# Quarters of the first modulation vectors: x loaded ahead of the weights, three blocks interleaved, and a 0/1 matrix in place of two transposes

## The chip, the cores and the metric

The kernel runs on one core of a Trainium2 chip. The metric is the device time of one execution in microseconds (us), as the median of several runs. All profile rows below come from one profiled execution, recorded by the hardware profiler.

## What is computed

One inference step through two layers of a diffusion backbone on 640 tokens of 1024 features (512 latent tokens and 128 context tokens, each group with its own conditioning vector). Per layer:

```
m = silu(cond) @ w_ada + b_ada
sh1, sc1, g1, sh2, sc2, g2 = split(m, 6)
h = rmsnorm(x) * (1 + sc1) + sh1
z = h @ w_in
branches: gated linear attention (4 heads), gated convolution, Fourier mixing
x += g1 * W_o(sum_b sigmoid(G_b) * W_b_out(branch_b))
h = rmsnorm(x) * (1 + sc2) + sh2
x += g2 * (silu(h @ w_gate) * (h @ w_up2)) @ w_down
```

and a last norm. All weights are float32, and nearly all of the time goes into streaming them and multiplying by them.

## The kernel before, in words

Everything is feature-major: a tile has 128 features on its partitions and all T = 640 tokens along its rows, so x is eight tiles of 128x640. The tokens go in two halves of 320 (TH).

**The weight stream.** `make_plan` (L816) lists every weight in the order of its use; `_load` (L127 to L136) issues the loads of 512 KB on the queue of SyncE (SP) into six buffers called raw; a buffer is free again when `take` (L175) has handed its weight out or its split is done. `prefetch` (L186) splits the weights that come next, up to two ahead: `_split` makes a rounded high part on ScalarE (`whi`, ACT L140) and the rest on VectorE (`wlo`, DVE L141), three buffers each. A dense product is done in three matmuls, high by high, low by high and high by low, each with a 128x128 block as the loaded operand and 320 tokens moving. A block of 128 outputs over eight feature blocks and both halves is so 8 x 3 x 2 = 48 matmuls (`dense` L242, or `mm3h` L224 to L226 by halves). Two blocks that are neighbours in the plan go as a `pair` (L244) in 84 matmuls by the scheme of Strassen and Winograd. It needs sums of the two halves of the tokens, which `token_sums` makes once per h: L290 to L293 on DVE, a high part `thi` on ACT (L301) and a low part `tlo` on DVE (L302).

**Modulation vectors.** They are made by pieces, a quarter of one vector at a time: 256 features for both conditioning vectors. `ada_mm` (L342) does 8 float32 matmuls with 32 columns loaded and 256 moving; their parts come out on four groups of 32 partitions, of which two rows each count. `ada_end` copies the 128x256 result to SBUF (ACT L348), transposes it in two blocks of 128x128 on TensorE (L351, `ident` is the identity), adds the four parts up with a reduction (DVE L354), adds b_ada (L355), and for the two scales makes A = (1 + sc) * norm (L358). It is called one piece late: `ada` does the products of a piece, then ends the piece before. There are 48 pieces: 8 in the start (sc1 and sh1 of layer 0, four quarters each), and 40 that the plan spreads among the pairs of the mixers and the FFN.

**The start** (`start`, L546). The stream's first six loads are issued, then x's eight. The first pieces are made while the norm is computed (squares on ACT and DVE, sum over features on PE at L409, 1/rms on ACT at L381), x is multiplied by it in eight DVE instructions (L565), and then, quarter by quarter, h is made by two activations per feature block (ACT L577), split in high and low (`hhl`, ACT L457 and DVE L455, L458), and fed to one block of the input projection, Q0. With it go the products `gk` (L541) of the low-rank gates. Q1, K0 and K1 (two blocks of 128 columns each make up Q and K) follow as dense blocks in `mixer` (L894); the token sums stand behind the call for K0. The first pair, `w1p_4`, is V's first two blocks; `w1p_6` is the next pair.

Which instruction of the program stands where on each engine is decided by a scheduler from priorities in program order; tiles come from pools (47 units of SBUF, four PSUM tiles of two banks), and an engine runs its own instructions strictly in the order given.

## Time and profile before

| what | number |
|---|---|
| runs (us) | 2076.96, 2074.67, 2073.61; median 2074.67 |
| span of the profiled execution (us) | 2075.0 |
| time of the profiled execution beside its span | none is given; the span stands 0.3 above the median |
| TensorE matmul (PE) busy | 2012.5 us, 97% |
| weight load (PEld) busy | 1936.3 us, 93% |
| VectorE (DVE) busy | 1570.5 us, 76% |
| ScalarE (ACT) busy | 919.4 us, 44% |
| read and written in HBM | 227.69 MB and 26.74 MB |

Busy time of PE is from the start of a matmul to its modelled end, so neighbours overlap; how fast it runs is read from the starts of neighbours. A row of the timeline has its start in us from the start of the span, the busy time, the engine, the line, the operation, the tiles out<-in with their shapes, how many instructions are put together (x2), and, in brackets, how long the engine was idle before it and what ended that.

### The profile page before, as it was taken

To read this page: it belongs to the slowest core of one execution; us is meant where nothing else is said; L and a number is where in the kernel's file an instruction comes from. 1 tells how busy PE (TensorE), PEld (TensorE's weight loads), DVE (VectorE), ACT (ScalarE), POOL (GpSimd) and SP (SyncE) were. 2 spreads that over 40 slices of the span, in tenths; PEclk is the share of its full clock that TensorE was granted. 3 is DMA by queue.
4 is the path that set the end of the run, shared out by engine and by line. 5 is a ranking of instruction groups with operands and counts; after the bars stand their busy time and mean duration, and the time that the engine had idled before them with its cause. 6 is when DMAs were issued, how large, how long until landed. Compare 5 with 4: busy or idle time off the path is not lost. (4 is left out here: it accounts for less than half of the span.)

```text
span 2075.0 us, 35216 instructions
## 1 busy us (share of the span) xinstructions
PE 2012.5 (97%) x14100; PEld 1936.3 (93%) x14100; DVE 1570.5 (76%) x2508; ACT 919.4 (44%) x1445; POOL 18.2 (1%) x52
## 2 busy tenths in 40 slices
PE   5999999999999999999999999999999999999997
PEld 2999998999999999999979999899999999999997
DVE  5778798877667777777677878898765787877876
ACT  5554435445445333333365454544543643333333
POOL 2000000000000000000000000000000000000000
PEclk9999999999999999999999999999999999999999
DMA  8254442554612333333232453335545222222222
GB/s 320 69 171 136 148 140 95 186 197 141 210 55 62 103 118 98 105 114 103 83 126 84 165 171 132 118 129 173 192 153 173 62 64 78 78 92 71 88 72 71
DMA packets 107139, 256.72 MB, mean 124 GB/s; under 512 B 13344, under 2 KB 46304, under 8 KB 106976
## 3 DMA queue, kind: packets, MB, share of 16 engines
q1 hardware_dynamic: 102528, 250.91, 36.8%
q8 instruction: 111, 1.82, 0.4%
q10 hardware_dynamic: 3728, 2.49, 0.4%
q0 software_dynamic: 720, 1.07, 0.1%
q14 instruction: 52, 0.43, 0.1%
HBM read 227.69 MB, written 26.74 MB: 123 GB/s over the span
## 5 line engine op out<-in xcount | busy, mean ns | idle before, releaser
L140 ACT CAST whi<-raw 128x1024 fp32r<-128x1024 f32 (+2 forms) x368 | 270.1, 734 | 529.5 <-PE wo L242 37.3
L141 DVE TENSOR_TENSOR wlo<-raw,whi 128x1024 fp32r<-128x1024 f32 (+2 forms) x368 | 304.4, 828 | 112.2 <-ACT whi L140 111.8
L242 PE MATMUL wd<-ffhi,whi 128*128 128x320 f32 x656 | 150.2, 310 | 0.0
L242 PE MATMUL wd<-fflo,whi 128*128 128x320 f32 x656 | 149.5, 309 | 0.0
L242 PE MATMUL wd<-ffhi,wlo 128*128 128x320 f32 x656 | 149.4, 309 | 0.0
L140 ACT CAST whi<-sb 128x1024 fp32r<-128x1024 f32 x86 | 90.3, 1050 | 125.7 <-PE wd L242 31.5
L140 ACT CAST whi<-sc 128x1024 fp32r<-128x1024 f32 x86 | 90.3, 1050 | 107.8 <-PE wd L242 48.0
L141 DVE TENSOR_TENSOR wlo<-sc,whi 128x1024 fp32r<-128x1024 f32 x86 | 104.9, 1220 | 30.2 <-ACT whi L140 29.6
L473 DVE SCALAR_TENSOR_TENSOR x<-wd,mod,x 128x512 f32<-128x512 f32 x212 | 106.7, 545 | 23.0 <-PE wd L242 23.0
L242 PEld LDWEIGHTS wd<-ffhi,whi 128*128 128x128 f32 x656 | 109.4, 188 | 3.3 <-ACT whi L140 3.3
L141 DVE TENSOR_TENSOR wlo<-sb,whi 128x1024 fp32r<-128x1024 f32 x86 | 104.8, 1219 | 6.8 <-ACT whi L140 6.7
L242 PEld LDWEIGHTS wd<-ffhi,wlo 128*128 128x128 f32 x656 | 109.7, 188 | 0.0
L242 PEld LDWEIGHTS wd<-fflo,whi 128*128 128x128 f32 x656 | 109.6, 188 | 0.0
L162 DVE TENSOR_TENSOR sc<-raw 128x512 f32<-128x512 f32 x86 | 59.3, 689 | 27.3 <-DMA raw<-in_w 26.0
L342 PE MATMUL ada<-raw,cond 128*32 128x256 f32 x768 | 56.5, 410 | 9.2 <-ACT cond L381 5.5
L163 DVE TENSOR_TENSOR sb<-sc,raw 128x512 f32<-128x512 f32 x86 | 59.1, 687 | 0.5
L168 DVE TENSOR_TENSOR sc<-raw,sb 128x512 f32<-128x512 f32 x86 | 59.1, 687 | 0.3
L242 PE MATMUL wb<-bhi,whi 128*128 128x320 f32 x256 | 59.2, 312 | 0.0
L164 DVE TENSOR_TENSOR sb<-raw,raw 128x512 f32<-128x512 f32 x86 | 59.0, 686 | 0.0
L242 PE MATMUL wb<-bhi,wlo 128*128 128x320 f32 x256 | 58.4, 309 | 0.0
L242 PE MATMUL wb<-blo,whi 128*128 128x320 f32 x256 | 58.3, 309 | 0.0
L342 PEld LDWEIGHTS ada<-raw,cond 128*32 128x32 f32 x768 | 20.8, 114 | 31.7 <-issue 7.2
(2254 smaller groups left out, 6417.0 us busy)
## 6 DMA issues: line engine op xcount, KB each, us to landing
raw<-in_w SPq DMA_DIRECT2D x104, 512.0 KB, 4.4
raw<-in_w_ada SPq DMA_DIRECT2D x96, 512.0 KB, 3.8
raw<-in_wu SPq DMA_DIRECT2D x88, 512.0 KB, 3.6
raw<-in_wd SPq DMA_DIRECT2D x96, 192.0 KB, 2.3
sgd<-z SPq DMA_DIRECT2D x48, 320.0 KB, 3.1
sgl<-sgd SPq DMA_DIRECT2D x48, 320.0 KB, 3.8
raw<-in_wb SPq DMA_DIRECT2D x48, 256.0 KB, 2.8
raw<-in_wo SPq DMA_DIRECT2D x16, 512.0 KB, 3.5
```

Of the source, the lines that this page charges most:

```text
L140: self.nc.scalar.copy(hi[:, 0:n], src)
L141: self.nc.vector.tensor_sub(lo[:, 0:n], src, hi[:, 0:n].bitcast(F32))
L162: nc.vector.tensor_add(sc[:, 0:512], a21, a22)
L163: nc.vector.tensor_sub(sb[:, 0:512], sc[:, 0:512], a11)
L164: nc.vector.tensor_sub(sb[:, 512:1024], a11, a21)
L168: nc.vector.tensor_sub(sc[:, 512:1024], a12, sb[:, 0:512])
L242: nc.tensor.matmul(o[h], w[:, sl], rhs[kb][h][part], start=(kb == 0 and first), stop=(kb == nk - 1 and last))
L342: self.nc.tensor.matmul(ps[32 * j:32 * j + 32, 0:256], self.cond[:, 4 * kp + j, :], r[:, j, :], start=(kp == 0), stop=(kp == 1))
L473: self.nc.vector.scalar_tensor_tensor(seg(xv), seg(v), g[:, j, i:i + 1], seg(xv), ALU.mult, ALU.add)
```

## The change

Four things are changed.

- `start` issues x's eight loads ahead of the weight stream, and the norm's instructions come first in the program. The pieces of sc1 and of sh1 of one quarter are made together in one PSUM tile (`vectors`), and h's multiplication by 1/rms moves into the loop over quarters.
- Three blocks instead of one, Q0, Q1 and K0, are fed quarter by quarter; their weights are loaded behind quarter 0 (Q0, Q1) and quarter 1 (K0) by the table `START_HEAD`. The gate products gk come after them in program order. Layer 1 keeps its two head blocks; its plan is written differently but names the same order.
- `ada_end` no longer transposes and reduces. A constant `sel`, 128x2, has a 1 where row p belongs to column p mod 32; a matmul with 128 columns of the copied result loaded and sel's two columns moving adds the four parts up and puts features on partitions at once. DVE adds b_ada straight from PSUM. The copy to SBUF now follows the products of the same piece, while the matmul with sel still comes one piece later outside the start.
- `prefetch` counts no raw weights (those of w_ada, which need no split) in its look-ahead of two.

```diff
@@ -34,6 +34,7 @@
 CTX = [4, 9]
 FF_CHUNKS = [(0, 3), (3, 3), (6, 3), (9, 3), (12, 3), (15, 3), (18, 4)]
 FF_PLAIN = (2,)
+START_HEAD = {0: [0, 1], 1: [2]}
 NFF = 22
 SH1, SC1, G1, SH2, SC2, G2 = range(6)
 
...
@@ -184,11 +185,11 @@
         return self.hl.pop(c)
 
     def prefetch(self, ahead):
         self._load()
         while self.prepped < len(self.chunks):
             j = self.chunks[self.prepped][0]
-            if sum(1 for q in range(self.used, self.prepped + 1) if self.chunks[q][1] != "d") > ahead:
+            if sum(1 for q in range(self.used, self.prepped + 1) if self.chunks[q][1] not in "dr") > ahead:
                 break
             if any((j, n) not in self.raw for n in range(len(self.plan[j][2]))):
                 break
...
@@ -301,11 +302,13 @@
         self.nc.scalar.copy(hi, src)
         self.nc.vector.tensor_sub(lo, src, hi.bitcast(F32))
 
     def consts(self):
         nc, cp, a = self.nc, self.cp, self.a
         self.ident = cp.tile([P, P], F32, name="ident")
         make_identity(nc, self.ident)
+        self.sel = cp.tile([P, 2], F32, name="sel")
+        nc.vector.tensor_reduce(self.sel, self.ident.rearrange("p (j i) -> p i j", j=4)[:, 0:2, :], op=ALU.add, axis=mybir.AxisListType.X)
         self.ones_d = cp.tile([P, P], F32, name="ones_d")
         nc.vector.memset(self.ones_d, 1.0 / D)
         self.ones_v = cp.tile([P, P], F32, name="ones_v")
...
@@ -335,49 +338,57 @@
             p["A2"] = cp.tile([P, KB, 2], F32, name=f"A2{l}")
             self.par.append(p)
 
-    def ada_mm(self, ps, kp, raw):
+    def ada_mm(self, o, kp, raw):
         r = raw.rearrange("p (k c) -> p k c", k=4)
         for j in range(4):
-            self.nc.tensor.matmul(ps[32 * j:32 * j + 32, 0:256], self.cond[:, 4 * kp + j, :], r[:, j, :], start=(kp == 0), stop=(kp == 1))
-
-    def ada_end(self, l, v, n, ps):
-        nc = self.nc
-        p = self.par[l]
-        u = self.unit(cols=256, s="adas")
-        nc.scalar.copy(u, ps[:, 0:256])
-        pm = ps[:, 512:768]
-        for k in range(2):
-            nc.tensor.transpose(pm[:, k * P:k * P + P], u[:, k * P:k * P + P], self.ident)
-        ks = slice(2 * n, 2 * n + 2)
-        mv = p["mod"][:, v, ks]
-        nc.vector.tensor_reduce(mv, pm.rearrange("p (k j i) -> p k i j", k=2, i=32)[:, :, 0:2, :], op=ALU.add, axis=mybir.AxisListType.X)
-        nc.vector.tensor_add(mv, mv, p["b_ada"][:, v, ks])
-        for w, A, norm in ((SC1, "A1", "norm1"), (SC2, "A2", "norm2")):
-            if v == w:
-                nc.vector.scalar_tensor_tensor(p[A][:, ks], mv, 1.0, p[norm][:, ks], ALU.add, ALU.mult)
+            self.nc.tensor.matmul(o[32 * j:32 * j + 32], self.cond[:, 4 * kp + j, :], r[:, j, :], start=(kp == 0), stop=(kp == 1))
+    def ada_make(self, ps, pieces):
+        for i, (l, v, n) in enumerate(pieces):
+            for kp in range(2):
+                self.ada_mm(ps[:, i * 256:i * 256 + 256], kp, self.take(("ada", l, v, n, kp)))
+        c = 256 * len(pieces)
+        u = self.unit(cols=c, s="adas")
+        self.nc.scalar.copy(u, ps[:, 0:c])
+        return u
+    def ada_end(self, ps, pieces, u):
+        nc = self.nc
+        for i in range(2 * len(pieces)):
+            nc.tensor.matmul(ps[:, 512 + 2 * i:514 + 2 * i], u[:, i * P:i * P + P], self.sel, start=True, stop=True)
+        for i, (l, v, n) in enumerate(pieces):
+            p = self.par[l]
+            ks = slice(2 * n, 2 * n + 2)
+            mv = p["mod"][:, v, ks]
+            pm = ps[:, 512 + 4 * i:516 + 4 * i].rearrange("p (k i) -> p k i", k=2)
+            nc.vector.tensor_add(mv, pm, p["b_ada"][:, v, ks])
+            for w, A, norm in ((SC1, "A1", "norm1"), (SC2, "A2", "norm2")):
+                if v == w:
+                    nc.vector.scalar_tensor_tensor(p[A][:, ks], mv, 1.0, p[norm][:, ks], ALU.add, ALU.mult)
 
     def ada(self, pieces):
-        for l, v, n in pieces:
+        for piece in pieces:
             ps = self.psum("ada")
-            for kp in range(2):
-                self.ada_mm(ps, kp, self.take(("ada", l, v, n, kp)))
+            u = self.ada_make(ps, [piece])
             self.ada_flush()
-            self.ada_last = l, v, n, ps
+            self.ada_last = ps, [piece], u
 
     def ada_flush(self):
         if self.ada_last:
             self.ada_end(*self.ada_last)
         self.ada_last = None
 
     def table(self, name):
         self.in_order(lambda: self.tc.keep_in_program_order(self.nc.scalar.preload_act_table_set(name)))
 
     def act(self, *args, **kw):
         self.in_order(lambda: self.nc.scalar.activation(*args, **kw))
 
     def in_order(self, make):
...
@@ -534,44 +545,49 @@
     def head_psum(self, head, gk):
         return [self.psum("_".join(map(str, k))) for k in ([] if gk is None else [("gk", gk)]) + head]
 
+    def gk_half(self, l, ps, half, ks):
+        for k in ks:
+            j = k % 4
+            self.nc.tensor.matmul(ps[32 * j:32 * j + 32, half * 512:half * 512 + TH], self.par[l]["wgk"][:, 32 * k:32 * k + 32],
+                                  self.hx[k][:, half * TH:half * TH + TH], start=(k < 4), stop=(k >= 4))
     def head_block(self, hps, hws, gk, kb, half):
         if gk is not None and kb % 4 == 3:
-            for k in range(kb - 3, kb + 1):
-                j = k % 4
-                self.nc.tensor.matmul(hps[0][32 * j:32 * j + 32, half * 512:half * 512 + TH], self.par[gk]["wgk"][:, 32 * k:32 * k + 32],
-                                      self.hx[k][:, half * TH:half * TH + TH], start=(k < 4), stop=(k >= 4))
+            self.gk_half(gk, hps[0], half, range(kb - 3, kb + 1))
         for ps, w in zip(hps[-len(hws):], hws):
             self.mm3h(ps, w, kb, self.hcur[kb], half, kb == 0, kb == KB - 1)
 
     def start(self, x, xs, A, sh, head):
         nc = self.nc
         h, hx = [], []
         self.hcur, self.hx = h, hx
-        self._load()
         for k in range(KB):
             xs.append(self.unit(s="x"))
             nc.sync.dma_start(xs[k], x[k])
+        self._load()
         self.table("natural_log_exp_and_others")
-        pieces = [[(0, SC1, n), (0, SH1, n)] for n in range(4)]
-        self.ada(pieces[0])
         for k in range(KB):
             self.sq_add(k, xs[k])
         for half in range(2):
             self.sq_sum(half)
         r = self.rstd_from(self.sq_ps)
-        for k in range(KB):
-            hx.append(self.unit(s="hx"))
-            nc.vector.tensor_mul(hx[k], xs[k], r)
-        hws = [self.take(k) for k in head]
-        self.ada(pieces[1])
-        hps = self.head_psum(head, 0)
+        hws = []
+        def vectors(n):
+            ps = self.psum("ada")
+            pieces = [(0, SC1, n), (0, SH1, n)]
+            self.ada_end(ps, pieces, self.ada_make(ps, pieces))
+            for k in START_HEAD.get(n, []):
+                hws.append(self.take(("w1", 0, k)))
+        vectors(0)
+        vectors(1)
+        hps = self.head_psum(head, None)
         for n in range(4):
-            if n < 2:
-                self.ada(pieces[n + 2])
-            else:
-                self.ada_flush()
             for k in (2 * n, 2 * n + 1):
+                hx.append(self.unit(s="hx"))
+                nc.vector.tensor_mul(hx[k], xs[k], r)
                 for i, seg in enumerate((lat, ctx_)):
                     o = seg(halves(hx[k]))
                     nc.scalar.activation(o, o, AF.Identity, scale=A[:, k, i:i + 1], bias=sh[:, k, i:i + 1])
...
@@ -580,18 +596,23 @@
                     self.split_half(half, hx[k], h[k])
             for half in range(2):
                 for k in (2 * n, 2 * n + 1):
-                    self.head_block(hps, hws, 0, k, half)
-        return h, hx, hps
-
+                    self.head_block(hps, hws, None, k, half)
+            if n < 2:
+                vectors(n + 2)
+        gk = self.psum("gk")
+        for half in range(2):
+            self.gk_half(0, gk, half, range(KB))
+        return h, hx, [gk] + hps
     def to_tokens(self, u):
         pt = self.psum("tt")
         for i in range(5):
             self.nc.tensor.transpose(pt[:, i * P:i * P + P], u[:, i * P:i * P + P], self.ident)
         return pt
 
     def gla_start(self, l):
         nc = self.nc
         nc.gpsimd.tensor_scalar_mul(self.par[l]["nb_gk"], self.par[l]["b_gk"], -1.0)
...
@@ -834,13 +855,11 @@
 
         for n in range(4):
             ada([(0, SC1, n), (0, SH1, n)])
-            if n == 0:
-                w1(0, Q0)
-        w1(0, Q0 + 1)
+            w1(0, *START_HEAD.get(n, []))
         for l in range(NL):
             if l:
-                w1(l, Q0, Q0 + 1)
-            w1(l, K0, K0 + 1)
+                w1(l, Q0, Q0 + 1, K0)
+            w1(l, K0 + 1)
             for i, (n, m) in enumerate(PAIRS):
                 w1p(l, n, m)
                 ada(ada_after(l, "mix", i))
...
@@ -931,8 +950,8 @@
                 yield from self.gla_head(l, hd, gk, twice(qk[Q0 + i], r), twice(qk[K0 + i], r), v, yo)
 
         qk_out(Q0, hps[1])
-        qk_out(Q0 + 1, hps[2] if l else self.dense(("w1", l, Q0 + 1), h))
-        ps = self.dense(("w1", l, K0), h)
+        qk_out(Q0 + 1, hps[2])
+        ps = self.dense(("w1", l, K0), h) if l else hps[3]
         T12, T34 = self.token_sums(hx)
         hx.clear()
         qk_out(K0, ps)
...
@@ -1005,7 +1024,7 @@
         dram = lambda s, n: [self.dp.tile([P, T], F32, tag=f"{s}{k}", name=f"{s}{k}") for k in range(n)]
         xd, self.sgd, self.ogd, self.fxd = dram("xd", KB), dram("sgd", 3 * KB), dram("ogd", 4), dram("fxd", 4)
         self.start_stream(self.make_plan())
-        head1 = [[("w1", l, Q0), ("w1", l, Q0 + 1)][:1 + l] for l in range(NL)]
+        head1 = [[("w1", l, n) for n in (Q0, Q0 + 1, K0)[:3 - l]] for l in range(NL)]
         xs = []
 
         def modulated(l, A, sh):
```

Lines of the changed kernel stand up to 19 lower than before; names in the order below have the tiles' numbers.

On ACT, at the start, before (rstd is 1/rms, adas the copied result of a piece, whi a weight's high part, hx the features' tile that becomes h, mod and A the modulation vectors):

```order
L381 ACTIVATE rstd_262<-ssq_259,eps 128x640
L381 ACTIVATE rstd_262<-rstd_262 128x640
L348 COPY adas_294<-ada_210 128x256
L348 COPY adas_313<-ada_283 128x256
L348 COPY adas_335<-ada_300 128x256
L348 COPY adas_354<-ada_322 128x256
L577 ACTIVATE hx_265<-hx_265,mod_107,A_108 128x2x256
```

and with the change:

```order
L392 ACTIVATE rstd_227<-ssq_224,eps 128x640
L141 CAST whi_231<-raw_0_196 128x1024
L392 ACTIVATE rstd_227<-rstd_227 128x640
L141 CAST whi_237<-raw_0_198 128x1024
L354 COPY adas_265<-ada_230 128x512
L354 COPY adas_305<-ada_282 128x512
L593 ACTIVATE hx_319<-hx_319,mod_109,A_110 128x2x256
L141 CAST whi_276<-raw_0_259 128x1024
L593 ACTIVATE hx_319<-hx_319,mod_109,A_110 128x2x64
```

Q0's, Q1's and K0's high parts (whi_231, whi_237, whi_276) now stand among the norm and the first activations, and quarter 1's copy (adas_305) stands ahead of the first activation of quarter 0.

On DVE, between the second and the third quarter with the change (hx_507, hx_517 and hx_563 are feature blocks 4, 5 and 6, hhl their high and low parts, sb and sc sums for the first pair's weights, ada_469 the PSUM tile of the last quarter's vectors):

```order
L590 TENSOR_TENSOR hx_507<-x_180,rstd_227 128x640
L163 TENSOR_TENSOR sc_703<-raw_1_470 128x512
L466 CAST hhl_511<-hx_507 128x320
L164 TENSOR_TENSOR sb_702<-sc_703,raw_0_398 128x512
L469 TENSOR_TENSOR hhl_511<-hx_507,hhl_511 128x320
L367 TENSOR_TENSOR mod_109<-ada_469,b_ada_92 128x4 x2
L370 SCALAR_TENSOR_TENSOR A_110<-mod_109,norm_94 128x4
L469 TENSOR_TENSOR hhl_514<-hx_507,hhl_514 128x320
L590 TENSOR_TENSOR hx_517<-x_182,rstd_227 128x640
L165 TENSOR_TENSOR sb_702<-raw_0_398,raw_1_470 128x512
L169 TENSOR_TENSOR sc_703<-raw_0_398,sb_702 128x512
L142 TENSOR_TENSOR wlo_769<-raw_1_470,whi_768 128x512
```

The addition out of ada_469 stands ahead of the rest of the third quarter's work; PE has the matmul that writes ada_469 behind all products of the second quarter.

On DVE, behind the blocks of the start, before (t are the token sums, tlo their low parts, wlo the weights' low parts):

```order
L141 TENSOR_TENSOR wlo_553<-raw_0_396,whi_552 128x1024
L290 TENSOR_TENSOR t_76_662<-hx_265 128x320
L141 TENSOR_TENSOR wlo_610<-raw_0_409,whi_609 128x1024
L291 TENSOR_TENSOR t_77_663<-hx_273,hx_265 128x320
L292 TENSOR_TENSOR t_76_662<-hx_273,t_76_662 128x320
```

and with the change:

```order
L469 TENSOR_TENSOR hhl_580<-hx_573,hhl_580 128x320
L142 TENSOR_TENSOR wlo_395<-raw_0_392,whi_394 128x1024
L142 TENSOR_TENSOR wlo_473<-raw_0_398,whi_472 128x1024
L142 TENSOR_TENSOR wlo_708<-sb_702,whi_707 128x1024
L291 TENSOR_TENSOR t_68_642<-hx_319 128x320
```

Three low parts (K1 and the first two of the pair `w1p_4`) now stand ahead of the first token sum, directly behind the last feature block's low part, where one stood before.

## Rows read from the trace of the kernel before

**Rows 1.** Windows over the span: us, then busy us of PE, PEld, DVE, ACT, POOL (x instructions), clock, DMA share, GB/s.

```profile
0.00:36.66 36.66, 13.75 (x110) 5.46 (x111) 16.61 (x33) 14.62 (x22) 10.89 (x26) 1.00 0.88 337
36.66:90.47 53.81, 53.75 (x346) 44.57 (x347) 40.05 (x79) 30.94 (x50) 2.06 (x5) 0.94 0.37 125
90.47:2075.00 1984.53, 1945.00 (x13646) 1886.24 (x13644) 1513.84 (x2398) 873.80 (x1374) 5.26 (x21) 1.00 0.37 120
```

**Rows 2.** Waits of PE: engine, line, what it waited for: us, times, longest.

```profile
PE ssq L409 <- DVE sq L398: 10.7, 1, 10.7
PE ada L351 <- ACT adas L348: 6.4, 3, 2.6
PE w1p_17a L224 <- DVE z L279: 4.1, 2, 2.3
```

**Rows 3.** The window of the first 19 us, and the page's queue of small loads.

```profile
0.00:19.00 19.00, 4.76 (x34) 1.10 (x34) 4.33 (x10) 6.53 (x9) 10.89 (x26) 1.00 0.87 327
...
q0 software_dynamic: 720, 1.07, 0.1%
```

**Rows 4.** Timeline of ACT in the start.

```profile
27.07 0.79 ACT L381 ACTIVATE rstd<-ssq,eps 128x640 f32<-128x640 f32 x1 [4.31 <-PE ssq L409]
28.54 0.80 ACT L348 COPY adas<-ada 128x256 f32<-128x256 f32 x2
...
34.96 1.91 ACT L577 ACTIVATE hx<-hx,mod,A 128x512 f32<-128x512 f32 x3 [3.23 <-DVE mod L355]
...
59.43 1.05 ACT L140 CAST whi<-raw 128x1024 fp32r<-128x1024 f32 x1 [1.09 <-PE w L225]
```

**Rows 5.** Timeline of DVE in the start.

```profile
28.67 5.97 DVE L565 TENSOR_TENSOR hx<-x,rstd 128x640 f32<-128x640 f32 x8 [4.19 <-ACT rstd L381]
34.56 0.17 DVE L354 TENSOR_REDUCE mod<-ada 128x4 f32<-128x16 f32 x1
...
36.19 0.33 DVE L455 CAST hhl<-hx 128x320 fp32r<-128x320 f32 x1 [0.49 <-ACT hx L577]
...
60.51 1.23 DVE L141 TENSOR_TENSOR wlo<-raw,whi 128x1024 fp32r<-128x1024 f32 x1 [3.99 <-ACT whi L140]
...
66.20 0.48 DVE L291 TENSOR_TENSOR t<-hx,hx 128x320 f32<-128x320 f32 x1
...
82.19 0.82 DVE L302 TENSOR_TENSOR tlo<-t,thi 128x640 fp32r<-128x640 f32 x1
```

**Rows 6.** Timeline of PE: the first block's beginning, and the starts of the first two pairs.

```profile
34.78 1.07 PE L342 MATMUL ada<-raw,cond 128*32 128x256 f32 x16 [2.69 <-DVE mod L354]
...
36.66 0.38 PE L224 MATMUL w<-hhl,whi 128*128 128x320 f32 x1 [0.44 <-DVE hhl L455]
...
42.27 0.47 PE L225 MATMUL w<-hhl,whi 128*128 128x320 f32 x1
42.54 0.47 PE L226 MATMUL w<-hhl,wlo 128*128 128x320 f32 x1
...
78.15 0.31 PE L224 MATMUL w1p_4a<-hhl,whi 128*128 128x320 f32 x1
...
90.47 0.31 PE L224 MATMUL w1p_6a<-hhl,whi 128*128 128x320 f32 x1
```

**Rows 7.** Timeline of PE around the two transposes of one piece in a pair.

```profile
128.17 0.31 PE L226 MATMUL w1p_30a<-thi,wlo 128*128 128x320 f32 x1
128.32 0.38 PE L351 MATMUL ada<-ident,adas 128*128 128x128 f32 x2
...
128.68 0.30 PE L225 MATMUL w1p_30c<-tlo,whi 128*128 128x320 f32 x1
```

**Rows 8.** Timeline of PE among the attention's float32 matmuls of few columns.

```profile
174.97 0.44 PE L686 MATMUL o<-am,v 128*128 128x128 f32 x2
175.25 0.56 PE L688 MATMUL o<-e,S 128*128 128x64 f32 x4
175.64 0.44 PE L686 MATMUL o<-am,v 128*128 128x128 f32 x2
```

## The prediction

> **What bounds the kernel now.** I read the windows first, cut where the program changes its kind: up to the first product of a projection block, from there to the second pair, and the rest. In the rest PE is busy 1945.00 of 1984.53 us at a granted clock of 1.00 [rows 1]: TensorE sets the time, and what is added to it there is paid unless it falls where PE waits. The first 36.66 us are another matter: PE is busy 13.75, the DMA engines 0.88 of the time. The waits of PE say for what: 10.7 us for the squares of x, whose loads stand behind six weights, then the copies and vectors of the first pieces; later the longest entry is 4.1 us for DVE's z in the pair 17 [rows 2]. The timelines of ACT and DVE show the chain that ends that stretch: 1/rms at 27.07, eight multiplications from 28.67 to 34.6, reduction, activation at 34.96, cast at 36.19, first product at 36.66 [rows 4 to 6]. So there are two sums to make: the start, from 0 to the second pair at 90.47 [rows 6], and the 40 pieces after it.
>
> **The start, up to the first product.** x is 2.62 MB. With quarter 0's four weights (2.10) and the small loads (1.07 and cond) it is 5.9 MB. Before, 6.21 MB came in 19 us (327 GB/s) and 12.35 in 36.66 [rows 1, 3], 0.35 MB per us between. So quarter 0 is there at about 18, Q0 and Q1 (7.0 MB) at 21, quarter 1's four (9.1 MB) at 27. The norm is no longer late. But ACT runs in its order: quarter 1's copy stands ahead of the first activation, so that one can't start before 27 + 0.5 of products + 0.6 of copy; then K0's high part (1.05 [rows 4]), the activation (0.65), K0's low part on DVE (1.14) and the cast: first product at about 32.0 instead of 36.66. That is 4.6 won.
>
> **The start, from there to the end of the heads.** Per quarter there are 2 feature blocks x 2 halves x 9 = 36 products, and 16 products of w_ada for the next pieces (1.07 [rows 6]). At the beginning of this stretch before, neighbours stood 0.27 us apart (42.27 and 42.54), and later 84 of them took 12.32 (78.15 to 90.47), 0.147 [rows 6]; these are the two levels of the clock, 1.2 and 2.4 GHz. Whether the lower one comes again here no row says, so I carry both: quarter 0 ends at 42.7 with the lower one for as many us as before, at 39.4 without.
> Quarter 1's products wait for copy, matmuls with sel, additions, activation, cast: 0.6 + 0.45 + 0.5 + 1.2 + 0.4, and for the second feature block another 2.9, under which 9 products lie; 27 follow (4.0). It ends at 52.9 or 49.6.
> Then comes the step that the order shows: DVE has the addition out of the last quarter's tile ahead of the rest of the third quarter, and PE writes that tile only behind quarter 1's last product. So from 52.9 there follow, on DVE alone, matmuls with sel 0.45, additions 0.5, a low part 0.4, a multiplication 0.74 (5.97 / 8 [rows 5]), three sums for the first pair and a small low part 1.85 (half of 1.23 [rows 5] each), a cast, a multiplication and a low part 1.45: 5.4 in which PE has 12 products. 60 products (8.8) follow: the heads end at 67.0 or 63.7.
>
> **The start, the token sums.** Three buffers hold high parts, and Q0, Q1 and K0 keep all three till the heads end. K1's and the first pair's splits follow only then: a cast 1.1 after the buffer is free [rows 4] and three low parts of 1.14 on DVE ahead of the first token sum, less 0.9 since Q0's last product comes early: 3.6. The sums took 16.8 us from 66.20 to 83.0 [rows 5]; one more sum and one weight sum stand among them now, 17.6 in all. The last low part is there at 88.2 or 84.9, and 36 products of the first pair need it or stand behind what does (5.3): second pair at 93.5 or 90.2, against 90.47. **+3.0 or -0.3; I take the middle, +1.4**, with -5 to +6 as bounds: without the wait for token sums it would be 63.7 + gk 1.9 + K1's 48 products 7.0 + 12.3 = 84.9, and +6 if quarter 1 runs at the lower clock as well (27 x 0.12 = 3.3).
>
> **The 40 pieces.** Removed per piece: two transposes with 128 columns moving, one record each, DVE's reduction (0.17 [rows 5]). From the product ahead of a pair of transposes to the second behind it are 0.51 us [rows 7]; less two steps of 0.147 the transposes cost 0.218. Added: two float32 matmuls with 128 columns loaded and 2 moving. No row has 2 columns. The nearest are the attention's: from 174.97 to 175.64 there are two records with 128 columns moving and four with 64, the latter two to an instruction: 0.67 / 6 = 0.112 per record, and 64 columns don't cost less than 128 [rows 8]. So what counts there is records, and float32 outside a transpose has two: 4 x 0.112 = 0.448 per piece, +0.230, +9.2 for 40. The other end is a record that costs in proportion to its columns, next to nothing: -0.218 x 40 = -8.7. I take the row's.
> The Trainium skill ("TensorE: Matmul & The Clock Gate", section "LDWEIGHTS (loading the stationary operand)") says that a weight load's time goes by the loaded columns, 107 ns for 128, whatever the matmul streams; by it a piece adds 4 x 0.107 - 0.218, and the 40 add 8.4, an estimate from that page. It speaks against this change, and the trace agrees in that 64 and 128 columns cost the same there.
> Not all is paid. The waits for z, 4.1 us at the pair 17 alone [rows 2], can take up lateness that gathers before them; z needs PE's own products, so I take a third of that, 1.5. And where PE waits for DVE, the missing reduction gives some 0.2 back at six places: 1.2. **+6.5.** Bounds 0 and +9.2.
>
> **What costs nothing.** The copy on ACT right behind a piece's products: ACT is busy 873.80 of 1984.53 [rows 1], and its order between splits stays as it was; if that cover is gone, a split is late by 0.4. The look-ahead without raw weights can make splits earlier only where a raw and a whi buffer are free, and the buffers are as many as before; a gain lies within the 40 us that PE has without work after the start [rows 1], of which I take none. The 0/1 matrix itself is one instruction on DVE in an idle stretch.
>
> **Sum.** 2075.0 (the profiled span, 0.3 above the median of the runs) + 1.4 + 6.5 = 2082.9, and I forecast 2083.
>
> **Rivals.**
> *The matrix is cheap (faster).* If a record's cost falls with its moving columns, the pieces give 0.218 x 40 = 8.7 back: 2075.0 + 1.4 - 8.7 = 2067.7. It decides at a record below 0.0545 us, where four cost what the two transposes did. For it: nothing is moved but two columns, and neighbours in a dense stream hide weight loads (PEld is 93% busy beside PE). Against it: the rows with 64 and 128 columns, and that load paths are as full as PE in the pairs. Chance 0.12.
> The Trainium skill (the same page, section "Back-to-back issue gap") gives 1 to 64 columns one price, some 60 cycles or 25 ns; by it four records cost 0.10, the pieces give back 4.7, and the sum is 2071.7, an estimate from that page. Rows 8 don't bear it out at 64 columns.
> *The lateness is absorbed.* PE is late by 0.2 a piece, but where pieces stand DVE or weights end the pair anyway. Then the steady term is 0 to 1, 2075.0 + 1.4 + 0.6 = 2077.0. For it: DVE is at 1513.84 of 1984.53, and z is waited for. Against it: PE has only 40 us without work in the whole stretch [rows 1]. Chance 0.14.
> *The start does win.* Should the scheduler's order leave the token sums no later than the heads, the second pair starts at 84.9, -5.5: 2075.0 - 5.5 + 6.5 = 2076.0. Against it: the three buffers. Chance 0.12.
> *The start does worse than it should.* The lower clock lasts through quarter 1, and the waits between quarters add up: 2075.0 + 6 + 9.2 = 2090. For it: more and longer gaps of PE ahead of each quarter than before. Chance 0.12.
>
> **How the numbers follow.** The forecast has 0.50 (its own range 2079 to 2088). A measurement of this kernel can tell 0.2%, about 4.1 us, from no change: faster is below 2070.5, slower above 2078.8. Slower: the forecast 0.50 and the worse start 0.12, 0.62. Faster: most of the cheap matrix, 0.10, and 0.04 of a winning start with part of the pieces absorbed, 0.14. The rest, 0.24, is within. The range from 2070 to 2091 leaves out the cheap matrix at its full price and little else.
>
> **What would show it.** In the changed profile: first product at about 32; a gap of PE of 3 to 6 us between the second and the third quarter, ended by DVE; three low parts of weights ahead of the first token sum, and PE waiting for tlo in w1p_4; w1p_6 at about 92. In the pairs, four records of L361 some 0.11 apart where two of L351 stood, so that neighbours stand 0.75 apart and not 0.51. I am wrong if two instructions of L361 cost 0.22 or less, if w1p_6 starts before 86, or if PE's wait time after the start falls by as much as the records add.

## The result, and the profile after

The changed kernel takes 2094.43 us (median of four executions, 2091.08 to 2097.09), against 2074.69 before: the ratio is 1.0091, 95% interval [1.0077, 1.0105], some 19 us slower. The profiled execution is the shortest of the four (2091.08, span 2089.2), and the one before was the longest of its own (2076.96, span 2075.0), so the two traces differ by 14.2 us and the medians by 19.7. One more execution of the changed kernel, the one profiled in the repeat below, took 11083 us at a mean granted clock of 0.166; it and its profile are left out of what follows. Which executions are long goes with the mean granted clock: 0.994 to 0.997 in twelve executions of the kernel before, 0.992, 0.991, 0.990 and 0.989 in 2091.08, 2094.10, 2094.77 and 2097.09 us of the changed one.

The windows of the changed kernel, cut at the first product, the end of the blocks in the start, the first pair and the second pair (columns as in [rows 1]):

```profile
0.00:35.12 35.12, 13.29 (x85) 7.35 (x85) 12.96 (x25) 15.74 (x21) 10.90 (x26) 0.86 0.94 335
35.12:73.19 38.07, 36.21 (x240) 27.27 (x244) 17.77 (x41) 13.98 (x26) 0.00 (x0) 0.91 0.47 150
73.19:82.93 9.74, 8.89 (x69) 7.73 (x70) 9.30 (x15) 6.29 (x10) 0.00 (x0) 1.00 0.33 109
82.93:100.72 17.79, 14.98 (x86) 13.68 (x85) 15.91 (x25) 10.09 (x13) 2.06 (x5) 0.90 0.11 31
100.72:2089.00 1988.28, 1953.43 (x13726) 1894.45 (x13724) 1509.62 (x2358) 874.79 (x1374) 5.27 (x21) 1.00 0.37 120
```

The second pair begins at 100.72 against 90.47 [rows 1, 6]: 10.25 of the 14.2 us are lost in the start, 3.9 in the rest (1988.5 us from there to the end, 1984.5 before). The first product is only 1.5 us earlier. From there to the second pair PE idles 5.5 us where it idled 0.06, and the clock is 0.91 and 0.90 in two stretches. The waits of PE:

```profile
PE ssq L420 <- DVE sq L409: 15.9, 1, 15.9
PE ada L361 <- ACT adas L354: 8.6, 5, 3.3
...
PE w1p_46d L225 <- DVE z L270: 3.6, 2, 1.9
PE w L225 <- DVE hhl L466: 3.1, 2, 1.9
...
PE w1p_4b L225 <- ACT thi L302: 1.4, 1, 1.4
```

The first entry holds no loss by itself: nothing of PE's stands ahead of the norm now. The copies (L354) are waited for longer than before [rows 2], and there are new waits at w1p_46d (the last of the four PSUM parts, a to d, of a pair in the mixer) and in the first pair, and longer ones in the heads. The start on PE, up to the second quarter's products:

```profile
18.34 3.55 PE L345 MATMUL ada<-raw,cond 128*32 128x256 f32 x32
25.21 1.86 PE L361 MATMUL ada<-sel,adas 128*128 128x2 f32 x8 [3.33 <-ACT adas L354]
27.01 3.64 PE L345 MATMUL ada<-raw,cond 128*32 128x256 f32 x32
31.35 1.87 PE L361 MATMUL ada<-sel,adas 128*128 128x2 f32 x8 [0.70 <-ACT adas L354]
35.12 1.17 PE L225 MATMUL w<-hhl,whi 128*128 128x320 f32 x3 [1.90 <-DVE hhl L466]
...
44.90 1.06 PE L345 MATMUL ada<-raw,cond 128*32 128x256 f32 x14
46.66 1.05 PE L361 MATMUL ada<-sel,adas 128*128 128x2 f32 x8 [0.70 <-ACT adas L354]
48.15 1.94 PE L345 MATMUL ada<-raw,cond 128*32 128x256 f32 x18 [0.44 <-PE ada L361]
50.02 1.17 PE L225 MATMUL w<-hhl,whi 128*128 128x320 f32 x3
51.12 1.66 PE L345 MATMUL ada<-raw,cond 128*32 128x256 f32 x10
```

and what ACT did ahead of quarter 0's copy:

```profile
22.06 1.04 ACT L141 CAST whi<-raw 128x1024 fp32r<-128x1024 f32 x1 [2.82 <-DMA raw<-in_w]
23.01 0.73 ACT L392 ACTIVATE rstd<-rstd 128x640 f32<-128x640 f32 x1
23.65 1.03 ACT L141 CAST whi<-raw 128x1024 fp32r<-128x1024 f32 x1
24.59 0.58 ACT L354 COPY adas<-ada 128x512 f32<-128x512 f32 x1
```

Quarter 0's products are done at 21.9, but their copy stands on ACT behind Q0's split, which waits for Q0's load, and behind Q1's: PE idles 3.33 us. Behind that gap eight records with the matrix take 1.86 us where they take 0.95 to 1.05 at the upper level of the clock. The 32 of w_ada behind it take 3.64, 0.114 per record against 0.067 in [rows 6]; but the 32 ahead of the gap take 3.55 as well, so this set is slow without the gap too (the view gives a clock of 1.00 there; the clock's records begin only at 21.7). Below is the granted clock in the three slow stretches of the start, and then the fourth load of quarter 1, which is issued at 21.96 and lands 6.4 us later, at 28.4:

```profile
25.20:38.60 13.40, 10.78 (x63) 6.78 (x64) 6.61 (x17) 4.74 (x8) 0.00 (x0) 0.50 0.93 326
49.10:52.30 3.20, 3.20 (x18) 1.44 (x14) 2.70 (x7) 1.66 (x3) 0.00 (x0) 0.50 0.89 315
93.40:96.70 3.30, 3.13 (x11) 2.78 (x12) 2.21 (x4) 2.69 (x3) 0.00 (x0) 0.50 0.16 27
...
L133 SPq DMA_DIRECT2D raw<-in_w_ada x1: 327/327/327, 22.0 to 22.0; - x1
DMA to landing us min/median/max: 6.4/6.4/6.4
```

The timeline of DVE at the token sums:

```profile
75.55 1.22 DVE L142 TENSOR_TENSOR wlo<-sb,whi 128x1024 fp32r<-128x1024 f32 x1
76.69 0.49 DVE L291 TENSOR_TENSOR t<-hx 128x320 f32<-128x320 f32 x1
...
93.06 0.82 DVE L303 TENSOR_TENSOR tlo<-t,thi 128x640 fp32r<-128x640 f32 x1
```

and that of PE in the first pair:

```profile
89.65 0.41 PE L226 MATMUL w1p_4a<-tlo,whi 128*128 128x320 f32 x1 [0.66 <-DVE tlo L303]
...
91.61 0.41 PE L225 MATMUL w1p_4b<-thi,whi 128*128 128x320 f32 x1 [1.41 <-ACT thi L302]
92.59 0.41 PE L226 MATMUL w1p_4b<-tlo,whi 128*128 128x320 f32 x1 [0.57 <-DVE tlo L303]
...
95.43 0.47 PE L226 MATMUL w1p_4c<-tlo,whi 128*128 128x320 f32 x1
95.70 0.47 PE L227 MATMUL w1p_4c<-thi,wlo 128*128 128x320 f32 x1
```

The last low part is there at 93.9, 10.9 us into a pair that began at 82.93; before it was 4.9 (83.0 and 78.15 [rows 5, 6]). The pair takes 17.8 us instead of 12.3: 2.8 of waits and, behind them, products 0.27 apart until 96.8.

A piece in the steady stretch, the same place as [rows 7]:

```profile
138.34 0.31 PE L227 MATMUL w1p_30a<-thi,wlo 128*128 128x320 f32 x1
138.49 0.50 PE L361 MATMUL ada<-sel,adas 128*128 128x2 f32 x4
...
139.09 0.31 PE L226 MATMUL w1p_30c<-tlo,whi 128*128 128x320 f32 x1
```

0.75 from the product ahead to the second behind, 0.51 before: +0.24 (the mean over the eight pieces of the first FFN is 0.23).

### The profile page after: what moved, and what is told of

Its sections match the earlier page's. It is cut to its first block, busy times and chain, and to the rows that moved or that the text cites. A ratio compares the mean times of both kernels' runs of the same rounds, so it can differ in the third digit from the quotient of the medians.

```text
span 2089.2 us, 35313 instructions
## 1 busy us (share of the span) xinstructions
PE 2026.8 (97%) x14196; PEld 1950.5 (93%) x14196; DVE 1565.6 (75%) x2461; ACT 920.9 (44%) x1441; POOL 18.2 (1%) x52
## 3 DMA queue, kind: packets, MB, share of 16 engines
q0 software_dynamic: 720, 1.07, 0.2%
## 4 chain that ended last, share of the span: by engine, by line
PE 81%; DVE 9%; issue 5%; ACT 3%; DMA 2%; SPq 0%; DVEq 0%; ACTq 0%; POOLq 0%
PE wd L243 14%; PE wb L243 8%; PE wo L243 3%; PE wu L243 2%; PE ada L345 2%; DVE wlo L142 2%; DVE S L688 1%; DMA raw<-in_w 1%; ACT whi L141 1%; PE ada L361 1%; PE wu L226 1%; PE wo L225 1%; PE wo L226 1%; PE wo L227 1%; PE wu L225 1%
## 5 line engine op out<-in xcount | busy, mean ns | idle before, releaser
L243 PEld LDWEIGHTS wb<-bhi,whi 128*128 128x128 f32 x256 | 42.0, 188 | 3.7 <-issue 0.9
```

Source lines behind the costliest of these rows:

```text
L243: nc.tensor.matmul(o[h], w[:, sl], rhs[kb][h][part], start=(kb == 0 and first), stop=(kb == nk - 1 and last))
```

## The experiments

All ratios are to the kernel before on the same chip, with their 95% intervals; positions are of the profiled execution.

**The matrix alone**, on the kernel before:

```diff
-            nc.tensor.transpose(pm[:, k * P:k * P + P], u[:, k * P:k * P + P], self.ident)
+            nc.tensor.matmul(ps[:, 512 + 2 * k:514 + 2 * k], u[:, k * P:k * P + P], self.sel, start=True, stop=True)
...
```

> Theory A (two sums: the pieces cost 0.23 us each in the pairs, the start costs 10): the start's order is the old one here, so the 40 pieces add 9.2 less what waits take up, and the 8 in the start at most 2: 2079 to 2084, and neighbours of a piece in the pairs stand 0.23 us further apart than before. Theory B (the matrix is cheap where nothing else waits, the loss sits in the start): 2070 to 2077.

2083.80, ratio 1.0043 [1.0029, 1.0056]: theory A, at its upper end. The steps of 0.23 are there; the rest is where the clock falls (a drop at 1064 to 1071 us that the trace of before has not). So the matrix costs by itself about what 40 x 0.23 = 9.2 say.

**The matrix 128 columns wide**, on the changed kernel:

```diff
-        self.sel = cp.tile([P, 2], F32, name="sel")
+        self.sel = cp.tile([P, P], F32, name="sel")
+        nc.vector.memset(self.sel, 0.0)
...
```

> The changed kernel with 126 columns of zeros added to the 0/1 matrix: 128 columns move instead of 2, in as many records. If a record costs by its loaded columns and not by the moving ones, nothing changes in the pairs: 0.23 more per piece than the transposes as before, 2092 to 2098. If moving columns have a price at all, up to 126/2.4 = 0.05 us x 4 per piece, and 8 us more: 2099 to 2104.

2090.35, 1.0079 [1.0066, 1.0092], no slower than the changed kernel and a little under the 2092 that was expected. The same place as above:

```profile
136.71 0.31 PE L227 MATMUL w1p_30a<-thi,wlo 128*128 128x320 f32 x1
136.86 0.60 PE L362 MATMUL ada<-sel,adas 128*128 128x128 f32 x4
...
137.45 0.31 PE L226 MATMUL w1p_30c<-tlo,whi 128*128 128x320 f32 x1
```

0.74 again. Between 2 and 128 moving columns there is nothing to pay where 128 are loaded: records count, and the rival of the cheap matrix falls.

**Transposes back, old look-ahead, late copies**, each alone undone in the changed kernel:

```diff
-            nc.tensor.matmul(ps[:, 512 + 2 * i:514 + 2 * i], u[:, i * P:i * P + P], self.sel, start=True, stop=True)
+            nc.tensor.transpose(ps[:, 512 + i * P:640 + i * P], u[:, i * P:i * P + P], self.ident)
...
```

> Theory A: the pieces' 4 to 7 us come back and, in the start, half of four times eight records at the lower clock (up to 3.6), less the reductions: 2085 to 2089, the second pair still starts at 97 to 100. Theory C (the matmuls with the matrix are the chain of the start: ACT copies, PE, DVE): nearly all comes back, 2073 to 2080, the second pair starts at 92 or before.

2091.94, 1.0086 [1.0072, 1.0099], second pair at 98.7: no clear difference to the changed kernel, and both theories miss the time. The steps of 0.23 do go, but PE then comes earlier to z and waits longer (4.8 us at w1p_46d, 3.6 in the changed kernel). In the profiled execution, the longest of its kernel, the granted clock also falls in six stretches behind the second pair's start, where the changed kernel's trace has one. Where PE waits for DVE, work taken off PE is not time won.

```diff
-            if sum(1 for q in range(self.used, self.prepped + 1) if self.chunks[q][1] not in "dr") > ahead:
+            if sum(1 for q in range(self.used, self.prepped + 1) if self.chunks[q][1] != "d") > ahead:
```

> The changed kernel with the old look-ahead, which counts raw weights. Theory A: the look-ahead only moves waits between places in the mixers, within 3 us of the changed kernel: 2091 to 2098. Theory D (splits that are made too early take raw or split buffers and slow the start): the start gets faster by more than 3 us, 2085 to 2090.

2089.23, 1.0074 [1.0061, 1.0086]. The start is unchanged (second pair at 101.2), so theory D falls, though the time lies in its range; theory A, that nothing is won, misses by 2 us. The wait at w1p_46d goes in both layers.

```diff
-            u = self.ada_make(ps, [piece])
+            self.ada_make(ps, [piece])
             self.ada_flush()
-            self.ada_last = ps, [piece], u
+            self.ada_last = ps, [piece]
...
```

> The changed kernel with the pieces' copies one piece late, in the 40 later pieces, and nothing else undone. Theory K: the steps ahead of pc (1.8 and 1.1 us there) go, the rest stays: 2089 to 2092. Rival (the copies only move waits, and a later copy makes PE wait for it): 2093 to 2097.

(the copy stands in `ada_end` again) 2092.34, 1.0086 [1.0072, 1.0100]: inconclusive. The steps ahead of pc (the mixer's product with the Fourier matrix) are gone, and so is a gain of 2.5 us at the beginning of each FFN.

**The look-ahead alone**, on the kernel before (the same line, the other way):

> The kernel before with the new look-ahead alone. Theory I (it lets DVE split a later pair's weights ahead of the z that the present pair waits for, as the new wait of 1.9 us at w1p_46d in both layers shows, and PE's clock drops behind such waits): the wait at w1p_46d appears here too, 2077 to 2082. Rival (that wait belongs to the earlier copies of the pieces, the look-ahead only moves waits): none there, 2073 to 2076.

2077.78, 1.0022 [1.0013, 1.0031], with the wait at w1p_46d: 4.5 us in two waits. DVE ahead of that place, of this kernel:

```profile
254.41 1.22 DVE L141 TENSOR_TENSOR wlo<-raw,whi 128x1024 fp32r<-128x1024 f32 x1
255.55 1.47 DVE L617 TENSOR_TENSOR_SCAN bc<-scanm,u 64x640 f32<-64x640 f32 x1
257.04 1.49 DVE L618 TENSOR_TENSOR_SCAN bc<-scanm,u 64x640 f32<-64x640 f32 x1
258.55 0.82 DVE L269 TENSOR_TENSOR z<-w1p_46b,s 128x640 f32<-128x640 f32 x1
```

and of the kernel before:

```profile
256.65 0.82 DVE L269 TENSOR_TENSOR z<-w1p_46b,s 128x640 f32<-128x640 f32 x1
257.38 1.47 DVE L617 TENSOR_TENSOR_SCAN bc<-scanm,u 64x640 f32<-64x640 f32 x1
258.89 1.49 DVE L618 TENSOR_TENSOR_SCAN bc<-scanm,u 64x640 f32<-64x640 f32 x1
...
261.36 1.22 DVE L141 TENSOR_TENSOR wlo<-raw,whi 128x1024 fp32r<-128x1024 f32 x1
```

A split of the next pair and two scans now stand ahead of the z that frees PE's PSUM tile. Theory I holds for this place; in layer 0 the granted clock is 0.50 from 259.3 to 262.8, directly behind the wait.

**x first alone**, on the kernel before:

```diff
-        self._load()
         for k in range(KB):
             xs.append(self.unit(s="x"))
             nc.sync.dma_start(xs[k], x[k])
+        self._load()
```

> x's eight loads ahead of the stream and nothing else of the change. If the wait for the squares of x was what bounded the first 36 us: the norm ends some 6 us earlier and the second pair starts 3 to 5 us earlier, 2069 to 2072. If the bytes bounded it (the first pieces and Q0 are then as late as x was): no difference, 2073 to 2077.

2079.39, 1.0025 [1.0015, 1.0036]: slower, which neither had. The first pieces now come at 15 us, the norm's squares still stand behind them in the program, and the first product comes at 40.1.

**Fewer blocks in the start.** One block:

```diff
-START_HEAD = {0: [0, 1], 1: [2]}
+START_HEAD = {0: [0]}
...
+        head1 = [[("w1", l, n) for n in (Q0, Q0 + 1, K0)[:(1, 2)[l]]] for l in range(NL)]
```

> The changed kernel with one block (Q0) in the start instead of three; Q1 and K0 follow as dense blocks. Theory F (three blocks in the start keep the three buffers of high parts, and the token sums come late for it): PE's waits for tlo and thi in w1p_4 go (2.8 us with the clock's drop behind them 1.8), second pair at 94 to 97, 2086 to 2091. Rival G (the start is slow by its order of loads and of ACT's queue up to the first product, whatever it feeds): second pair at 99 or later, 2092 to 2097.

2084.14, 1.0049 [1.0037, 1.0061]; first product at 29.8, second pair at 87.3. More came back than theory F had: half of the whole loss was in the number of blocks. The windows of this kernel:

```profile
29.83:74.99 45.16, 44.85 (x304) 33.87 (x305) 32.51 (x65) 23.57 (x38) 0.00 (x0) 0.96 0.52 176
74.99:87.31 12.32, 12.32 (x86) 12.32 (x85) 12.23 (x19) 8.37 (x10) 2.06 (x5) 1.00 0.15 43
```

The first pair takes 12.32 again: Q1 and K0, now dense blocks between the last of h and the pair, cover the token sums (last low part at 80.6, 5.6 into the pair).

Two blocks, `{0: [0, 1]}`:

> The changed kernel with two blocks (Q0, Q1) in the start, both loaded behind quarter 0. Theory F (the third block takes the last buffer of high parts, and K1's and the first pair's splits and with them the token sums wait): most of the 10 us between three blocks and one come back, 2084 to 2087, second pair at 88 to 91. Theory J (each block ahead of the copies on ACT, and each 48 products that wait for h, costs its share): half, 2088 to 2091, second pair at 92 to 96.

2086.78, 1.0053 [1.0038, 1.0069]; second pair at 92.9 in a profiled execution that was the longest of its kernel. The time lies in theory F's range, the position in J's.

**Four split buffers**, with 44 units, and the control with 44 units alone:

```diff
-        c, sfx, b = (512, "2", 1) if small else (1024, "", 3)
+        c, sfx, b = (512, "2", 1) if small else (1024, "", 4)
...
```

> The changed kernel with four instead of three buffers each for high and low parts, and 44 instead of 47 units to make room. Theory F: K1's split is done before the blocks of the start end, the token sums start 1 to 2.5 us earlier against the kernel with 44 units and three buffers, the second pair 2 to 6 earlier. Theory J: within 1 us of it.

> The control for the four buffers: the changed kernel with 44 units. If no unit is waited for in the start, the second pair stands at 98 to 101 as with 47; later in the program fewer units may cost something: 2093 to 2100.

2095.11, 1.0099 [1.0085, 1.0112], against 2092.14, 1.0083 [1.0070, 1.0096]. The first token sum is at 74.9 and 73.3, the second pair at 99.5 and 97.1. Theory F falls as to the buffers: with a fourth the scheduler put another low part of the pair ahead of the sums, three as before.

**The blocks' weights behind quarter 1**:

```diff
-START_HEAD = {0: [0, 1], 1: [2]}
+START_HEAD = {1: [0, 1, 2]}
...
```

> The changed kernel with Q0, Q1 and K0 loaded behind quarter 1 instead of behind quarter 0 and 1. Theory H (the copy of quarter 0 waits on ACT behind Q0's split, and PE idles 3.3 us and falls to the lower clock): the copy comes at 22 instead of 24.6, quarter 1's products end 2 to 4 us earlier, the first block's product at 32 to 34, 2088 to 2092. Rival (the bytes set the first product, and Q0 now comes last): 35 or later, 2093 to 2098.

2091.62, 1.0078 [1.0063, 1.0094]. ACT now copies quarter 0 at 21.01 and the first product comes at 29.9, 5.2 earlier and earlier than theory H had. The edit moves two things, though: with Q0 and Q1 behind it, quarter 1's fourth load lands at 25.4 (issued at 19.57) and not at 28.4, and PE waits for these loads:

```profile
21.56 0.64 PE L345 MATMUL ada<-raw,cond 128*32 128x256 f32 x8 [0.63 <-DMA raw<-in_w_ada]
...
L133 SPq DMA_DIRECT2D raw<-in_w_ada x1: 328/328/328, 19.6 to 19.6; - x1
DMA to landing us min/median/max: 5.8/5.8/5.8
```

So ACT's queue and the order of the loads share the 5.2 us, and this run does not part them. The second pair comes at 95.3, and the first pair still takes 18.4. So with the same first product as with one block, three blocks end 8 us later.

**PE's gaps filled**, in the changed kernel and in the one before:

```diff
+    def warm(self, o, n):
+        for _ in range(n):
+            self.nc.tensor.matmul(o, self.ident, self.ones_d, start=True, stop=True)
...
```

> The changed kernel with idle PE time in the start filled by float32 matmuls of constants (14 between quarter 0's products and the matrix, 9 ahead of the first block, 4 each in two more places); what they write is overwritten before it is read. Theory A2 (PE's gaps between the quarters bring the lower clock, which costs some 5 us of the start): the first block's product comes at 32 to 33 instead of 35.1, the second pair at 94 to 97 instead of 100.7, mean clock 0.993 or more, 2087 to 2091. Rival E (the gaps are waits for ACT, DVE and loads, and the clock only stretches work that lies in them): the second pair within 1 us of 100.7, or later by what the filling takes, 2093 to 2098.

2095.83, 1.0102 [1.0088, 1.0117], and no test of the clock ahead of the matrix: the filling itself waited for ACT's copy and then delayed the matrix by its own 5.8 us.

```profile
25.42 5.83 PE L547 MATMUL ada<-ones_d,ident 128*128 128x128 f32 x28 [3.87 <-ACT adas L354]
31.08 0.95 PE L361 MATMUL ada<-sel,adas 128*128 128x2 f32 x8
```

What it shows is the price of the level: the eight records take 0.95 behind it, 1.86 without. From the filling's end to the first pair the clock stays up, and from the first product (39.34) to the first pair (85.27) pass 45.9 us where the changed kernel has 47.8 with the lower clock in parts: the clock's price there is some 2 us, or a little more, since 8 records of filling stand in the 45.9. The time and the second pair, at 102.95, are rival E's.

> The kernel before with 12 float32 matmuls of constants in PE's gap of 2.7 us ahead of the first block. If that gap brings the lower clock from 36 to 44 us and nothing else does: the first block's products stand 0.15 apart from the start, second pair at 87 to 88.5, 2070 to 2073. Rival (the clock falls later or elsewhere instead, or the products wait for h anyway): 90 to 91, 2073 to 2077.

In the profiled execution exactly that: the first product at 36.15, its neighbours 0.15 apart, the second pair at 87.0. In the median nothing, 2074.04, 0.9997 [0.9988, 1.0005]: either the drop from 36 to 44 us is not in every execution, or the filling costs what it wins; the kernel before has one trace only, which leaves this open. In that of the look-ahead alone, whose start has nearly the same order, the lower clock lasted from 34.1 to 37.5, half as long and mostly ahead of the first product (36.51), and the second pair stands at 87.6.

**What is left without blocks, matrix and look-ahead**: the kernel with one block, with transposes; then also with the old look-ahead; then also with late copies (the edits above together).

> The changed kernel with one block in the start and with transposes and reduction instead of the 0/1 matrix: of the change there remain x first, the earlier copies and the look-ahead. If the parts add up (three blocks 10 us, pieces 5 to 9): 2075 to 2079. Rival (with three blocks the transposes gave back only 2.5, so the pieces' price is mostly absorbed and what remains sits in the look-ahead and the copies): 2080 to 2084.

> The same with the old look-ahead: x first, quarters' vectors made together and earlier copies are left. The second pair stood at 87.3 with one block, 3.2 before the kernel before, and nothing else is dearer: 2069 to 2073. Rival (the earlier copies themselves cost the middle as much): 2075 to 2079.

> One block in the start, transposes, the old look-ahead, and the pieces' copies one piece late as in the kernel before: of the change only x first and the quarters' order in the start are left. With the earlier copies this start had the second pair at 88.2, and the mixer then lost 2.9 and 4.0 us ahead of pc in the two layers, where PE waits for a vector and for a reload. Theory K (these losses come from the earlier copies): they go, 2069 to 2073. Rival (they come from how the stages fall against each other, or the clock falls elsewhere): 2074 to 2078.

In this order: 2082.92, 1.0037 [1.0022, 1.0051]; 2076.57, 1.0011 [1.0003, 1.0020]; 2074.42, 0.9998 [0.9989, 1.0007]; each time in the rival's range. With late copies the losses ahead of pc go (2.9 and 4.0 us), as theory K had it, but so does the gain of 2.5 us at each FFN. The last has the first product 7.8 us and the second pair 2.0 us earlier than before and is no faster in the median. No version beat the kernel before.

**The changed kernel again:**

> The changed kernel once more, for a second profile and more times of it: 2091 to 2097, second pair at 98 to 101, and the lower clock in the start in the same three places (ahead of the first block, between the first two quarters, in the first pair) if the gaps bring it, in others if it falls by chance.

2092.69 (median of the four executions compared), 1.0083 [1.0070, 1.0096]: the time is as expected. For the second pair and the places of the clock this run gives nothing; the traces of the other experiments do. All nine traces of kernels with three blocks in the start, the changed one and eight variants, show the lower clock somewhere between 22 and 41 us and again within the first pair, and so does the one with two blocks; of the nine with one block or with the start of the kernel before, none shows it in the first pair. So the drop in the first pair goes with the number of blocks and is not chance. The one at 49 to 52 us is in two of the nine.

So the parts, put on one after the other:

| kernel | ratio | second pair at, us |
|---|---|---|
| before | 1 | 90.5 |
| x first, one block by quarters | 0.9998 [0.9989, 1.0007] | 88.4 |
| + copies at once | 1.0011 [1.0003, 1.0020] | 88.2 |
| + look-ahead | 1.0037 [1.0022, 1.0051] | 89.7 |
| + matrix | 1.0049 [1.0037, 1.0061] | 87.3 |
| + second block | 1.0053 [1.0038, 1.0069] | 92.9 |
| + third block (the change) | 1.0091 [1.0077, 1.0105] | 100.7 |

Two steps are clear of their intervals' overlap: the look-ahead (some 5 us) and the third block (some 8; with the repeat's 1.0083 some 6). In this order the matrix adds 2.5 and by itself 9; the parts don't add up. That they share PE's waits for DVE is a likely reason, which no run here isolates.

## Why the prediction was wrong

The sign was right, the size was not: 2083 was forecast, with 2091 as the upper end, and 2094.4 came. Most of the miss is in the term of the start: +1.4 with +6 as its upper bound, and +10.25 in the trace. Taken part by part (the middle where the forecast has two ends), the first product is 3.1 us late, quarter 0 takes 0.8 longer, quarter 1 3.2, the rest of the heads 0.7, the token sums 0.5 less, and the end of the first pair 1.5 longer: 8.8 of the 8.9 us.

- **The pieces, "4 x 0.112 = 0.448 per piece, +0.230"**: right, 0.24 and 0.23 in the trace, and what counts is records. By the Trainium skill ("TensorE: Matmul & The Clock Gate", section "LDWEIGHTS (loading the stationary operand)") a weight load's time goes by the loaded columns; the trace agrees in that the wide matrix, with the same 128 loaded, costs 0.74 against 0.75; no run varied the loaded columns. The 25 ns that its section "Back-to-back issue gap" gives for up to 64 columns are, by the same section, for a matmul without the load of its weights; these records, 0.11 us each, load theirs. The rest of the program is 3.9 us longer in the trace, where +6.5 was forecast with bounds 0 and 9.2. The medians leave some 9 for it, if the start costs the same in other executions, which no second profile shows.
- **"First product at about 32.0": this step failed**, 35.12. (Its own terms add up to 31.3, with a cast of 0.33.) From quarter 1's copy on it was right, 4.4 us where 4.5 were forecast; but that copy comes at 30.71 and not at 27.5. 1.4 of it are bytes: the fourth load lands at 28.4 and not at 27. The rest is that the forecast took the first copies as free once their loads were there, and gave quarter 1's products 0.5 us behind the last load. Quarter 0's copy stood behind Q0's split and its load: a gap of 3.3, then the matrix and 32 records of w_ada at the lower clock, which end at 30.65, 2.3 behind the last load. The forecast named ACT's order, but only for quarter 1's copy.
- **Quarter 1, 10.2 us: mis-sized**, 13.4 (45.0 to 58.4). The forecast names "16 products of w_ada for the next pieces (1.07)" per quarter; a quarter has two pieces, 32 records, and 1.07 is the time of 16. The end of quarter 0 at 39.4 has them all (32.0 + 5.3 + 2.1), but the chain of quarter 1 has none. Between 44.90 and 52.7 PE spends 42 such records, 4.7 us, half of that at the lower clock.
- The third step, the addition of the last quarter ahead of DVE's own work, was right in length: 58.4 to 73.2 is 14.8, 14.2 forecast. Its sign, a gap of PE of 3 to 6 us, is not there: 12 records of gk stand in it (from 60.7 on), and PE idles 0.7 us between 60 and 68.
- **Token sums**: 3.5 us between the heads' end and the first sum (3.6 forecast) and 17.2 long (17.6). But they end where the heads' lateness puts them, 93.9 and not 88.2, and then the waits bring the clock down once more: from the last low part to the second pair 6.8 and not 5.3.
- **The clock, carried as "both" for the first block alone**: in the start it is at the lower level in three stretches (25 to 39, 49 to 52 and 93 to 97 us), and in the executions later too. By their mean clocks (0.995 before, 0.991 after) up to 8 of the 19 us go with it: 0.001 of the mean is 1.9 us between the changed kernel's 2089.4 at 0.993 and 2097.1 at 0.989. How much of this the clock costs, and how much it only accompanies longer waits, no run parts. The sum had no term for it in the rest of the program.
- **"The look-ahead without raw weights": costed at nothing, and it costs some 5 us.** It was looked for as a gain, while the order of DVE moved a split and two scans ahead of a z that PE waits for.

The nearest rival was "the start does worse than it should" (2090), with the right place and too small a price: +6 for the start, where the trace has +10.25.

## What to carry to other kernels

Work that is moved forward also leaves the place where it was: Q1 and K0 as dense blocks were what covered the token sums, and with three blocks interleaved with their inputs PE had 9.7 us of other work behind them (73.2 to 82.9) while DVE was at splits and sums for 20.6 us (73.3 to 93.9). On an engine that runs in order, put no instruction that waits for a late load (a split of a weight) ahead of a short one on which another engine's chain hangs (a copy). And a float32 matmul with few moving columns is priced here by its records: before a reduction is moved to the engine that bounds the kernel, count the records there.

## What the runs showed of the hardware

A float32 matmul with 128 loaded columns takes two records of 0.11 us in a dense stream, with 2, 64 or 128 moving columns alike; a float32 transpose takes one. At the lower level of the clock eight such records take 1.86 us, at the upper 0.95. Gaps of TensorE of 1.4 to 3.9 us (at 22 and 90 us in the changed kernel, at 32 in the one before, at 30 in that with the look-ahead alone) were followed, at their end or some 2 us later, by 3.4 to 13.7 us at 1.2 GHz; the stretch at 49 us stands behind gaps of only 0.7 and 0.4. What that cost hung on how long it lasted and what stood there: 6.8 us over products in one execution of nearly the same start (second pair at 90.5), 3.4 us mostly ahead of the first product in another (87.6). So between two traces of such a kernel 3 us can be the clock's, and only medians over several executions compare them.
